# A two-layer hybrid trunk kernel on one core: first two phases pinned to the text's order, weights in idle tiles of h, GpSimd issues the later modulations' loads, TensorE makes one part of them

## The chip, the cores and the metric

The kernel runs on one core of one Trainium2 chip. The metric is device time in microseconds (us), the median over several runs; one further run was taken with the profiler and left the trace that is read here.

## What is computed

Two layers of a diffusion backbone, for 128 context tokens (`x_prompt`) and 256 latent tokens (`x_sample`), all in float32, width D = 2048. Each layer first makes a modulation from a condition vector (one for the context, one for the latents), then normalizes, scales and shifts its input by it, projects it, mixes, projects back and adds the result with a gate:

```python
for layer in range(DEPTH):
    sh_p, sc_p, gt_p = _adaln(c_ctx, w_mod, b_mod)       # silu(cond) @ w_mod + b_mod, split in 3
    sh_s, sc_s, gt_s = _adaln(c[:, None, :], w_mod, b_mod)
    h_p = _modulate(y_prompt, norm_g, sh_p, sc_p)        # rmsnorm(x) * (1 + scale) + shift
    h_s = _modulate(y_sample, norm_g, sh_s, sc_s)
    ...
    # layer 0: h @ l0_w_in (2048 x 7680), HGRN2 scan and dense attention, @ l0_w_out
    # layer 1: h @ l1_w_in (2048 x 5120), windowed attention, @ l1_w_out
    y_prompt = y_prompt + gt_p * out_p
    y_sample = y_sample + gt_s * out_s
```

Each modulation matrix `w_mod` is 2048 x 6144, 50 MB, and is used for two vectors only, so making a modulation is mostly a matter of loading it.

## The kernel before, in words

All 384 tokens are held together. A product `h @ w` is made in three matmuls on float32r halves (`whi` x `hh`, `whi` x `hl`, `wlo` x `hh`): the weights are loaded raw by SyncE (SP), ScalarE (ACT) rounds them to `whi`, VectorE (DVE) makes the rest `wlo`, and TensorE (PE) multiplies. `w_piece` does this for 512 KB of weights (a wlo of 128x1024).

**The start.** The first six groups of 512 columns of `l0_w_in` cannot start before the modulation of layer 0 is there. So the 16 tiles of 128 rows of h (k = 0 to 15) are taken in five phases, `START = ((0, 1), (1, 3), (3, 6), (6, 10), (10, 16))`. While the products of one phase run (`start_products`: six groups, 12 matmuls of 384 columns for each k), `start_mod` makes the modulation for the k of the next one: it loads 512 KB pieces of `l0_w_mod` (`mraw`, in the four buffers of the tag "raw"), multiplies them on PE with the two conditions (matmuls with 32 columns of weights, in four column groups of the array), copies the sums out (`ev`), transposes them, adds them up on DVE (`ms`, then `modc` and `acol`), and modulates x to `hh` and `hl` (`modulate`). These are called P0 to P4 below, P4 having 432 matmuls.

**The later modulations** (shift and scale of layer 1, the gates of both) are made by DVE in stretches of free time: `mod_acc` loads 16 pieces of 128x1024 (`mraw`, `MRAWB` = 3 buffers) and adds each in two operations, one for each condition, to `acc`; a `mod_part` then sums `acc` over the partitions on PE with four matmuls of 512 columns and four transposes. They stand in the list `mods`; `pump` runs a unit of them after each piece of weights, at `pace[1]` units a piece, when an account of DVE's and PE's time allows it. There are four parts, `mod_part(1, k0)` with k0 = 16, 24, 0, 8, then the gates.

**The order on an engine** is not that of the text: a scheduler lets each engine's instruction go when it thinks its inputs ready, with priorities. Each engine, SP and GpSimd (POOL) included, works through its queue in order, and an instruction that waits holds all behind it. POOL has the six `rpow` steps of the norms (line 444), loads of states, tables and x, and stores.

Of the kernel before, what the change touches and what calls it, by code (L numbers as in the profile page):

```python
# [14 lines left out]
P = 128  # L15
# [7 lines left out]
RATE0 = 0.6  # L23
# [22 lines left out]
def trunk_kernel(ctx: ExitStack, tc: tile.TileContext, I, O):  # L46
# [70 lines left out]
    queue, due, pace = [], [], [0.0, 0.0]  # L117

# [144 lines left out]
    def mod_acc(l, c0):  # L263
# [196 lines left out]
    def modulate(l, q, xt, rb, hq=None, parts=((0, 4),)):  # L460

        hh, hl = hq_tiles(q) if hq is None else hq
        for k0, k1 in parts:
            x = xt[:, k0:k1]
            nc.vector.tensor_tensor(out=x, in0=x, in1=rb.unsqueeze(1).broadcast_to([P, k1 - k0, T]), op=ALU.mult)
            for k in range(k0, k1):
                for c, s in CT:
                    kt = 4 * q + k
                    nc.scalar.activation(xt[:, k, s], xt[:, k, s], AF.Identity, bias=modc[l][:, kt, c:c + 1],  # L469
                                         scale=acol[l][:, kt, c:c + 1])  # L470
            nc.scalar.copy(hh[:, k0:k1], x)  # L471
            nc.vector.tensor_tensor(out=hl[:, k0:k1], in0=x, in1=hh[:, k0:k1].bitcast(F32), op=ALU.subtract)
        return hh, hl
# [232 lines left out]
    h0 = [hq_tiles(q) for q in range(4)]  # L706
# [13 lines left out]
    def start_group(acc, c0, k0, k1, copy):  # L720

        ps = [psm.tile([P, 512], F32, tag="mm", name=nm("mm")) for _ in range(4)]
        for kt, n in pairs(k0, k1):
            hi, lo = w_piece(spool, "sraw", SRAW, W0, kt, n, c0, 512)
            hh, hl = h0[kt // 4]
            for c in range(4):
                for k in range(n):
                    kq = kt % 4 + k
                    wh, wl = hi[:, k, c * P:c * P + P], lo[:, k, c * P:c * P + P]
                    nc.tensor.matmul(ps[c][:, 0:T], lhsT=wh, rhs=hh[:, kq], start=(kt + k == k0), stop=False)  # L730
                    nc.tensor.matmul(ps[c][:, 0:T], lhsT=wh, rhs=hl[:, kq], start=False, stop=False)
                    nc.tensor.matmul(ps[c][:, 0:T], lhsT=wl, rhs=hh[:, kq], start=False, stop=(kt + k == k1 - 1))
# [47 lines left out]
    for i, (k0, k1) in enumerate(phases):  # L780
# [6 lines left out]
        for j, _ in enumerate(start_products(k0, k1)):  # L787
            while done < (j + 1) * n_nxt // n:
                next(nxt, None)
                done += 1  # L790
# [462 lines left out]
```

## Time and profile before

| | us |
|---|---|
| median of 3 runs (1355.13 to 1356.93) | 1356.29 |
| the profiled execution | 1356.77 |
| its span, first to last instruction | 1355.0 |
| PE busy in the span | 1321.0 (97%) |
| DVE busy | 1019.0 (75%) |
| ACT busy | 647.9 (48%) |
| POOL busy | 72.4 (5%) |

The busy time of PE is the union of its matmuls, whose ends are modelled, so 97% says that PE rarely had nothing in flight, not that it ran at its peak. 1.8 us of the execution lie outside the span.

### The profile page before, as it was taken

To read this page: it belongs to the slowest core of one execution; us is meant where nothing else is said; L and a number is where in the kernel's file an instruction comes from. 1 tells how busy PE (TensorE), PEld (TensorE's weight loads), DVE (VectorE), ACT (ScalarE), POOL (GpSimd) and SP (SyncE) were. 2 spreads that over 40 slices of the span, in tenths; PEclk is the share of its full clock that TensorE was granted. 3 is DMA by queue.
4 is the path that set the end of the run, shared out by engine and by line. 5 is a ranking of instruction groups with operands and counts; after the bars stand their busy time and mean duration, and the time that the engine had idled before them with its cause. 6 is when DMAs were issued, how large, how long until landed. Compare 5 with 4: busy or idle time off the path is not lost.

```text
span 1355.0 us, 19101 instructions
## 1 busy us (share of the span) xinstructions
PE 1321.0 (97%) x7093; PEld 1125.7 (83%) x7093; DVE 1019.0 (75%) x1602; ACT 647.9 (48%) x1297; POOL 72.4 (5%) x84
## 2 busy tenths in 40 slices
PE   5899999999999999999999999999999999999998
PEld 4678888997888878787987887888888999998887
DVE  5678757998998745896998969995656664499743
ACT  4532233476655534755433347345766763352221
POOL 1000000000000021101000000200000101000000
PEclk8899999999999999999999999999999999999999
DMA  9989989755555334576778854784332345457642
GB/s 284 304 289 331 317 289 319 236 160 179 176 174 181 97 106 138 167 232 201 242 244 254 297 184 133 234 283 119 92 94 81 104 118 166 129 181 254 210 152 84
DMA packets 138317, 265.42 MB, mean 196 GB/s; under 512 B 8944, under 2 KB 46768, under 8 KB 138224
## 3 DMA queue, kind: packets, MB, share of 16 engines
q1 hardware_dynamic: 132592, 246.52, 56.9%
q0 software_dynamic: 5376, 17.60, 4.5%
q8 instruction: 56, 0.92, 0.3%
q14 instruction: 37, 0.30, 0.1%
q10 hardware_dynamic: 256, 0.08, 0.0%
HBM read 256.04 MB, written 8.13 MB: 195 GB/s over the span
## 4 chain that ended last, share of the span: by engine, by line
PE 91%; DMA 4%; DVE 3%; ACT 1%; POOL 1%; issue 0%; DVEq 0%; ACTq 0%; SPq 0%; POOLq 0%
PE mm L77 77%; PE px L77 14%; DMA raw<-in_l_w_in_dram 2%; DMA mraw<-in_l_w_mod_dram 1%; DVE wlo L77 1%; DVE acc L77 1%; DMA tB<-in_x_sample_dram 0%; ACT whi L370 0%; POOL sm L444 0%; DVE tB L77 0%; DMA rowc<-in_c_dram 0%; DVE tG L77 0%; ACT tE L469 0%; DVE tH L77 0%; POOL r L444 0%
## 5 line engine op out<-in xcount | busy, mean ns | idle before, releaser
L370 ACT CAST whi<-raw 128x1024 fp32r<-128x1024 f32 (+1 forms) x270 | 278.4, 1032 | 500.1 <-PE mm L77 393.7
L77 DVE TENSOR_TENSOR wlo<-raw,whi 128x1024 fp32r<-128x1024 f32 (+1 forms) x270 | 323.4, 1198 | 188.0 <-PE mm L77 148.6
L77 PE MATMUL mm<-whi,hh 128*128 128x512 f32 x1008 | 398.9, 396 | 0.0
L77 PE MATMUL mm<-wlo,hh 128*128 128x512 f32 x1008 | 391.7, 391 | 3.2 <-DVE wlo L77 3.2
L77 PE MATMUL mm<-whi,hl 128*128 128x512 f32 x1008 | 393.5, 391 | 0.6 <-DVE hl L77 0.6
L77 DVE SCALAR_TENSOR_TENSOR acc<-mraw,csil,acc 128x1024 f32<-128x1024 f32 x240 | 299.0, 1279 | 9.0 <-DMA mraw<-in_l_w_mod_dram 9.0
L77 PE MATMUL mm<-hh,whi 128*128 128x384 f32 x768 | 264.4, 347 | 7.1 <-ACT hh L471 4.6
L77 PE MATMUL mm<-hl,whi 128*128 128x384 f32 x768 | 259.2, 338 | 0.0
L77 PE MATMUL mm<-hh,wlo 128*128 128x384 f32 x768 | 254.5, 338 | 0.2 <-DVE wlo L77 0.2
L77 PEld LDWEIGHTS mm<-wlo,hh 128*128 128x128 f32 x1008 | 189.3, 188 | 42.7 <-DVE wlo L77 5.8
L77 PEld LDWEIGHTS mm<-whi,hl 128*128 128x128 f32 x1008 | 189.3, 188 | 40.8 <-DVE hl L77 1.5
L77 PEld LDWEIGHTS mm<-whi,hh 128*128 128x128 f32 x1008 | 189.4, 188 | 39.3 <-ACT tE L824 0.8
L77 PEld LDWEIGHTS mm<-hh,whi 128*128 128x128 f32 x768 | 145.3, 190 | 22.2 <-issue 10.1
L77 PEld LDWEIGHTS mm<-hh,wlo 128*128 128x128 f32 x768 | 144.8, 189 | 2.7 <-DVE wlo L77 1.0
L77 PEld LDWEIGHTS mm<-hl,whi 128*128 128x128 f32 x768 | 145.5, 190 | 1.2 <-issue 0.2
L623 ACT ACTIVATE p<-px,nb,rs 128x384 f32<-128x384 f32 (+1 forms) x72 | 42.4, 596 | 15.0 <-DVE nb L77 14.5
L77 PE MATMUL px<-mraw,cs 128*32 128x256 f32 (+1 forms) x576 | 40.4, 377 | 4.9 <-DMA mraw<-in_l_w_mod_dram 4.9
L633 ACT ACTIVATE p<-p,sum 128x384 f32<-128x384 f32 (+1 forms) x72 | 36.1, 540 | 15.1 <-DVE sum L77 13.2
L77 DVE TENSOR_REDUCE mx<-px 128x1 f32<-128x384 f32 (+1 forms) x54 | 29.7, 567 | 9.3 <-PE px L77 8.9
L77 PEld LDWEIGHTS px<-mraw,cs 128*32 128x32 f32 x576 | 16.3, 114 | 20.0 <-issue 8.2
L77 PEld LDWEIGHTS px<-ct,p 128*128 128x128 f32 x168 | 20.1, 141 | 8.3 <-issue 2.8
L444 POOL TENSOR_TENSOR rs<-rs,nhalf 128x12 f32<-128x12 f32 x6 | 14.7, 2450 | 227.5 <-DVE rs L77 227.5
(415 smaller groups left out, 1228.5 us busy)
## 6 DMA issues: line engine op xcount, KB each, us to landing
raw<-in_l_w_in_dram SPq DMA_DIRECT2D x194, 512.0 KB, 3.9
mraw<-in_l_w_mod_dram SPq DMA_DIRECT2D x192, 512.0 KB, 5.0
raw<-in_l_w_out_dram SPq DMA_DIRECT2D x64, 512.0 KB, 4.9
raw<-in_l_w_in_dram SPq DMA_DIRECT2D x12, 256.0 KB, 6.6
tK<-in_l_b_mod_dram POOLq DMA_DIRECT2D x6, 256.0 KB, 6.0
y1d<-tA POOLq DMA_DIRECT2D x2, 768.0 KB, 5.2
tD<-y1d POOLq DMA_DIRECT2D x2, 768.0 KB, 6.0
tL<-y1d POOLq DMA_DIRECT2D x2, 768.0 KB, 6.2
```

What stands on the lines that cost most here:

```text
L77: return f(*a, **k)
L370: nc.scalar.copy(hi, raw)
L444: nc.gpsimd.tensor_tensor(out=out, in0=out, in1=nhalf[:, 0:out.shape[1]], op=ALU.pow)
L623: nc.scalar.activation(p[:, j], ss[j], AF.Exp, bias=nb[:, j:j + 1], scale=rs[:, i + j:i + j + 1], accum_out=sm[:, j:j + 1])
L633: nc.scalar.activation(p[:, j], p[:, j], AF.Copy, scale=sm[:, j:j + 1])
```

## The change

Seven things change. `pin` keeps P0's and P1's matmuls on PE and weight loads on SP (with the modulation work that runs beside them, that is of k = 0 to 5) in the order of the text. The eight modulation pieces of k = 1, 2 go to the six idle tiles of h and two of the four "raw" buffers. The multiplication of x with `rb0` stands ahead, and `modulate` works on one k at a time; for a phase's first k ACT writes `hh` straight from x. `pace[1]` is 0 in P0. The last piece of modulation work of a phase comes one or two pieces of weights earlier (`n`). `mod_acc` loads are issued by POOL, inside `tc.issue_after(last_w[0].ins)`. And `mod_part(1, 8)` on DVE is replaced by `late_mod(1, 8)` on PE, beside P4's products.

```diff
-RATE0 = 0.6
+RATE0 = (0.0, 0.6, 0.6, 0.6, 0.6)
...
+    def pin(ins, queue):
+
+        if pinned[queue]:
+            tc.keep_in_program_order(ins)
+        return ins
...
             raws.append(wpool.tile([P, 1024], F32, tag="mraw", bufs=MRAWB, name=nm("mraw")))
-            nc.sync.dma_start(raws[kt], I[f"l{l}_w_mod"][kt * P:kt * P + P, c0:c0 + 1024])
+
+            with tc.issue_after(last_w[0].ins):
+                nc.gpsimd.dma_start(raws[kt], I[f"l{l}_w_mod"][kt * P:kt * P + P, c0:c0 + 1024])
...
-        nc.sync.dma_start(raw, w_view(w, kt, nk, c0, n))
+        ins = pin(nc.sync.dma_start(raw, w_view(w, kt, nk, c0, n)), "s")
+        if pinned["s"]:
+            last_w[0] = ins
...
+    def modulate(k, first):
+
+        x, (hh, hl) = xT[k // 4][:, k % 4], [t[:, k % 4] for t in h0[k // 4]]
+        for c, s in CT:
+            m, a = modc[0][:, k, c:c + 1], acol[0][:, k, c:c + 1]
+            nc.scalar.activation(hh[:, s] if first else x[:, s], x[:, s], AF.Identity, bias=m, scale=a)
+            if first:
+                nc.vector.tensor_scalar(out=x[:, s], in0=x[:, s], scalar1=a, scalar2=m, op0=ALU.mult, op1=ALU.add)
+        if not first:
+            nc.scalar.copy(hh, x)
+        return nc.vector.tensor_tensor(out=hl, in0=x, in1=hh.bitcast(F32), op=ALU.subtract)
...
-    h0 = [hq_tiles(q) for q in range(4)]
+
+    h0 = [hq_tiles(0)]
+    done0 = []
+    idle = ["hh1", "hl1", "hh2", "hl2", "hh3", "hl3"]
...
-                    raw = wpool.tile([P, k8, n], F32, tag="raw", bufs=RAWB, name=nm("mraw"))
-                    nc.sync.dma_start(raw, w_view(I["l0_w_mod"], k8 * i, k8, D * (1 - part) + k * P, n))
+                    if k == 1 and idle:
+                        raw = hpool.tile([P, 4 * T], F32, tag=idle.pop(0), name=nm("mraw"))[:, 0:1024]
+                        raw = raw.rearrange("p (k c) -> p k c", k=k8)
+                    else:
+                        raw = wpool.tile([P, k8, n], F32, tag="raw", bufs=RAWB, name=nm("mraw"))
+                    pin(nc.sync.dma_start(raw, w_view(I["l0_w_mod"], k8 * i, k8, D * (1 - part) + k * P, n)), "s")
...
+    def late_mod(l, k0):
+
+        for k in (k0, k0 + 4):
+            ps = px()
+            for i in range(8):
+                raw = wpool.tile([P, 2, 512], F32, tag="raw", bufs=RAWB, name=nm("mraw"))
+                nc.sync.dma_start(raw, w_view(I[f"l{l}_w_mod"], 2 * i, 2, k * P))
+                for kt in (2 * i, 2 * i + 1):
+                    nc.tensor.matmul(ps[32 * (kt % 4):32 * (kt % 4) + 32, :],
+                                     lhsT=cs32[:, kt, :], rhs=raw[:, kt % 2], start=(kt < 4), stop=(kt >= KT - 4))
+                yield
+            ev = mpool.tile([P, 512], F32, tag="t2", bufs=T2B, name=nm("ev"))
+            nc.scalar.copy(ev, ps)
+            cp = px()
+            for b in range(4):
+                nc.tensor.transpose(cp[:, b * P:b * P + P], ev[:, b * P:b * P + P], ident)
...
-    mods += [mod_part(1, k0) for k0 in (16, 24, 0, 8)] + [mod_gates(0, 0, "KL", ready0)]
-    pace[1] = RATE0
+    mods += [mod_part(1, k0) for k0 in (16, 24, 0)] + [mod_gates(0, 0, "KL", ready0)]
+    pinned["t"] = pinned["s"] = True
...
+            nxt, n_nxt = late_mod(1, 8), 16
+
+        n = len(first) * len(pairs(k0, k1)) - (2 if i == 0 else 1)
```

What this makes of the engines' queues is seen at three places. The first is the head of POOL's queue. Before, it holds three small loads and then the power step of the first norm (`r_239`), which all of the start waits for:

```order
L205 DMA rowb<-in_lb_gamma_dram 48x128
L219 DMA onh<-in_l_a_onorm_dram 128x1
L221 DMA nsink<-in_l_c_sink_dram 128x16
L444 ISA
L444 TENSOR_TENSOR r_239<-r_239,nhalf 128x1 x3
```

Of the change, the same place:

```order
L282 DMA mraw_677<-in_l_w_mod_dram 128x1024
L282 DMA mraw_679<-in_l_w_mod_dram 128x1024
L282 DMA mraw_796<-in_l_w_mod_dram 128x1024
L214 DMA rowb<-in_lb_gamma_dram 48x128
L228 DMA onh<-in_l_a_onorm_dram 128x1
L230 DMA nsink<-in_l_c_sink_dram 128x16
L282 DMA mraw_910<-in_l_w_mod_dram 128x1024
L457 ISA
L457 TENSOR_TENSOR r_239<-r_239,nhalf 128x1 x3
L282 DMA mraw_1015<-in_l_w_mod_dram 128x1024
```

The loads of the first later part stand at the very head, four of them before the norm's power step; the `issue_after` that names a load of SP has put none of them behind anything on POOL.

The second place is DVE from the sums of the first modulation (`ms`, k = 0) to the first `hl`, which P0's matmuls need. Before:

```order
L77 TENSOR_REDUCE ms_314<-px_311 128x4
L77 TENSOR_TENSOR wlo_332<-raw_328,whi_330 128x512
L77 TENSOR_TENSOR modc_122<-ms_314,par 128x2 x2
L77 TENSOR_TENSOR tG_187<-tG_187,rb_238 128x768
L77 SCALAR_TENSOR_TENSOR acol_124<-modc_122,par 128x2
L77 TENSOR_TENSOR tH_217<-tH_217,rb_238 128x768
L77 TENSOR_TENSOR wlo_365<-raw_361,whi_363 128x512
L77 TENSOR_TENSOR tH_217<-tH_217,rb_238 128x768
L77 TENSOR_TENSOR hl_43_255<-tE_133,hh_42_254 128x384
```

Of the change:

```order
L77 TENSOR_REDUCE ms_309<-px_306 128x4
L77 SCALAR_TENSOR_TENSOR acc_676<-mraw_1015,csil,acc_676 128x1024
L77 TENSOR_TENSOR modc_122<-ms_309,par 128x2 x2
L77 SCALAR_TENSOR_TENSOR acc_676<-mraw_1015,csil,acc_676 128x1024
L77 SCALAR_TENSOR_TENSOR acol_124<-modc_122,par 128x2
L77 SCALAR_TENSOR_TENSOR acc_676<-mraw_1093,csil,acc_676 128x1024
L77 TENSOR_SCALAR tE_133<-tE_133,acol_124,modc_122 128x128
L77 SCALAR_TENSOR_TENSOR acc_676<-mraw_1093,csil,acc_676 128x1024
L77 TENSOR_SCALAR tE_133<-tE_133,acol_124,modc_122 128x256
L77 SCALAR_TENSOR_TENSOR acc_676<-mraw_1269,csil,acc_676 128x1024
L77 TENSOR_TENSOR hl_43_255<-tE_133,hh_42_254 128x384
```

Five `acc` operations of a later part have moved in between; in the whole queue of the change all 32 of that part stand before the 12th `wlo`, the end of P1's, where before they were spread from the 4th to the 29th.

The third place is PE in P4, where one piece of weights ends and the next begins. Before:

```order
L77 MATMUL mm_2095<-hh_48_260,whi_2128 128x384
L77 MATMUL mm_2095<-hl_49_261,whi_2128 128x384
L77 MATMUL mm_2095<-hh_48_260,wlo_2130 128x384
L77 MATMUL mm_2092<-hh_48_260,whi_2162 128x384
L77 MATMUL mm_2092<-hl_49_261,whi_2162 128x384
```

Of the change:

```order
L77 MATMUL mm_2100<-hh_344_1866,whi_2135 128x384
L77 MATMUL mm_2100<-hl_345_1867,whi_2135 128x384
L77 MATMUL mm_2100<-hh_344_1866,wlo_2137 128x384
L77 MATMUL px_2163<-mraw_2164,cs_109 32x512 x2
L77 MATMUL mm_2097<-hh_344_1866,whi_2170 128x384
L77 MATMUL mm_2097<-hl_345_1867,whi_2170 128x384
```

Two matmuls of `late_mod` stand between the pieces, and so 16 times in P4, with four transposes after the 8th and the 16th time.

## Rows read from the trace of the kernel before

**Rows 1.** The page, part 1: busy us (share), instructions.
```profile
PE 1321.0 (97%) x7093; PEld 1125.7 (83%) x7093; DVE 1019.0 (75%) x1602; ACT 647.9 (48%) x1297; POOL 72.4 (5%) x84
```
**Rows 2.** Stretches: length, busy of each engine, PE clock, DMA share, GB/s.
```profile
core 0: us, PE busy (x) PEld busy (x) DVE busy (x) ACT busy (x) POOL busy (x), PEclk, DMA share, GB/s
30.00:215.00 185.00, 175.62 (x1268) 144.13 (x1261) 125.05 (x193) 65.10 (x103) 0.60 (x1) 0.97 0.93 309
...
215.00:290.00 75.00, 75.00 (x433) 74.99 (x433) 71.20 (x75) 41.51 (x50) 1.43 (x2) 1.00 0.70 231
290.00:1355.00 1065.00, 1054.44 (x5267) 895.24 (x5265) 803.37 (x1286) 528.58 (x1113) 66.77 (x71) 1.00 0.55 172
```
**Rows 3.** The chain that ended last, pieces: start us, us, what.
```profile
30.50 7.64 PE mm L77 x36
...
57.97 11.24 PE mm L77 x48
...
87.33 4.11 PE mm L77 x22
...
214.79 107.85 PE mm L77 x576
...
289.96 32.68 PE mm L77 x144
```
**Rows 4.** Order of time, PE alone, around a `mod_part`'s four matmuls.
```profile
322.25 0.39 PE L77 MATMUL mm<-whi,hl 128*128 128x512 f32 x1
322.57 1.07 PE L77 MATMUL px<-acc,ct 128*32 128x512 f32 x8
323.57 0.50 PE L77 MATMUL mm<-whi,hh 128*128 128x512 f32 x1
323.90 0.39 PE L77 MATMUL mm<-wlo,hh 128*128 128x512 f32 x1
```
**Rows 5.** The same around eight matmuls of `start_mod`, and its transposes.
```profile
147.90 0.34 PE L77 MATMUL mm<-hh,wlo 128*128 128x384 f32 x1
148.17 1.07 PE L77 MATMUL px<-mraw,cs 128*32 128x256 f32 x16
149.17 0.44 PE L77 MATMUL mm<-hh,whi 128*128 128x384 f32 x1
...
213.16 0.66 PE L77 MATMUL px<-ct,ev 128*128 128x128 f32 x4 [0.71 <-ACT ev L756]
```
**Rows 6.** DVE's work on `mraw` until 345 us: ns min/median/max.
```profile
L77 DVE SCALAR_TENSOR_TENSOR acc<-mraw,csil,acc x69: 1273/1279/1286, 36.0 to 340.2; 128x1024 f32<-128x1024 f32 x69
```
**Rows 7.** Stretches of the front, columns as in Rows 2.
```profile
0.00:20.00 20.00, 10.77 (x55) 8.10 (x55) 10.32 (x33) 9.31 (x26) 3.58 (x10) 0.98 0.94 273
20.00:26.00 6.00, 4.02 (x69) 3.08 (x73) 5.14 (x9) 1.37 (x3) 0.00 (x0) 0.77 0.76 222
...
64.00:72.00 8.00, 8.00 (x73) 7.46 (x73) 5.97 (x10) 1.32 (x2) 0.29 (x1) 1.00 0.29 89
72.00:92.00 20.00, 19.76 (x149) 16.48 (x151) 16.00 (x28) 5.28 (x7) 0.31 (x1) 1.00 1.00 343
```
**Rows 8.** The loads of `mod_acc` until 92 us, on SP's queue.
```profile
L271 SPq DMA_DIRECT2D mraw<-in_l_w_mod_dram x7: 367/477/1356, 25.1 to 71.4; - x7
```
**Rows 9.** Order of time, DVE: sums of k = 0, then its `hl`.
```profile
25.28 0.17 DVE L77 TENSOR_REDUCE ms<-px 128x4 f32<-128x16 f32 x1
...
29.38 0.55 DVE L77 TENSOR_TENSOR hl<-tE,hh 128x384 fp32r<-128x384 f32 x1
```
**Rows 10.** Loads of 256 KB on SP's and POOL's queue: median us to landing.
```profile
raw<-in_l_w_in_dram SPq DMA_DIRECT2D x12, 256.0 KB, 6.6
...
mkf<-in_masks_dram POOLq DMA_DIRECT2D x1, 256.0 KB, 6.6
```
**Rows 11.** The chain that ended last, from 290 to 490 us, by engine and line.
```profile
by line: PE mm L77 78.0%; PE px L77 22.1%
```
**Rows 12.** A stretch of the first layer's output projection, columns as in Rows 2.
```profile
700.00:760.00 60.00, 57.89 (x263) 46.47 (x262) 54.78 (x58) 24.92 (x45) 5.10 (x8) 1.00 0.81 255
```

More of the change, by code (lines that the diff above doesn't have):

```diff
@@ L744, in start_mod @@
             ps = px()
+            for i in range(k, k + nk):
+                x = xT[i // 4][:, i % 4]
+                if k:
+                    with tc.issue_after(done0[0].ins):
+                        nc.vector.tensor_tensor(out=x, in0=x, in1=rb0, op=ALU.mult)
+                else:
+                    nc.vector.tensor_tensor(out=x, in0=x, in1=rb0, op=ALU.mult)
             for part in range(2):
                 for i in range(2 * nk):
-                    raw = wpool.tile([P, k8, n], F32, tag="raw", bufs=RAWB, name=nm("mraw"))
-                    nc.sync.dma_start(raw, w_view(I["l0_w_mod"], k8 * i, k8, D * (1 - part) + k * P, n))
+                    if k == 1 and idle:
+                        raw = hpool.tile([P, 4 * T], F32, tag=idle.pop(0), name=nm("mraw"))[:, 0:1024]
+                        raw = raw.rearrange("p (k c) -> p k c", k=k8)
+                    else:
+                        raw = wpool.tile([P, k8, n], F32, tag="raw", bufs=RAWB, name=nm("mraw"))
+                    pin(nc.sync.dma_start(raw, w_view(I["l0_w_mod"], k8 * i, k8, D * (1 - part) + k * P, n)), "s")
                     for j in range(k8):
                         kt = k8 * i + j
-                        nc.tensor.matmul(ps[32 * (j % 4):32 * (j % 4) + 32, part * n:part * n + n],
-                                         lhsT=cs32[:, kt, :], rhs=raw[:, j], start=(kt < 4), stop=(kt >= KT - 4))
+                        pin(nc.tensor.matmul(ps[32 * (j % 4):32 * (j % 4) + 32, part * n:part * n + n],
+                                             lhsT=cs32[:, kt, :], rhs=raw[:, j], start=(kt < 4), stop=(kt >= KT - 4)), "t")
                     if part == 0 or i < 2 * nk - 1:
@@ L766, in start_mod @@
                 mod_cols(0, KT * (1 - part) + k, nk, sums[:, nk * part:nk * part + nk, :])
[L767 to L768 removed]
+            for i in range(k, k + nk):
+                if len(h0) <= i // 4:
+                    h0.append(hq_tiles(i // 4))
+                m = modulate(i, i == k0)
+                done0.append(m)
+            yield
+    def late_mod(l, k0):
[7 more added lines that the diff above has]
+                                     lhsT=cs32[:, kt, :], rhs=raw[:, kt % 2], start=(kt < 4), stop=(kt >= KT - 4))
+                yield
+            ev = mpool.tile([P, 512], F32, tag="t2", bufs=T2B, name=nm("ev"))
[3 more added lines that the diff above has]
+                nc.tensor.transpose(cp[:, b * P:b * P + P], ev[:, b * P:b * P + P], ident)
+            sums = spool.tile([P, 8], F32, tag="ms", bufs=2, name=nm("ms")).rearrange("p (b c) -> p b c", c=2)
+            nc.vector.tensor_reduce(
+                out=sums, in_=cp.rearrange("p (b j r) -> p b r j", j=4, r=32)[:, :, 0:2, :], axis=AX.X, op=ALU.add)
+            mod_cols(l, k, 4, sums)
     def start_products(k0, k1):
@@ L783, in trunk_kernel @@
             k2, k3 = phases[i + 1]
-            nxt, n_nxt = start_mod(k2, k3), 4 * (k3 - k2)
-        n = len(first) * len(pairs(k0, k1))
+            nxt, n_nxt = start_mod(k2, k3), 4 * (k3 - k2) + len(pairs(k2, k3))
+        else:
+            nxt, n_nxt = late_mod(1, 8), 16
+        n = len(first) * len(pairs(k0, k1)) - (2 if i == 0 else 1)
         done = 0
         for j, _ in enumerate(start_products(k0, k1)):
-            while done < (j + 1) * n_nxt // n:
+            while done < min(n_nxt, (j + 1) * n_nxt // n):
                 next(nxt, None)
```

26 lines of the change are left out of this document (8 added, 18 removed).

## The prediction

> **What bounds the kernel now.** I read the page's busy times first: TensorE 97%, VectorE 75% [rows 1]. A modelled 97% could still hide waits, so next come the stretches. From 290 us to the end TensorE is idle for 1065 - 1054.4 = 10.6 us, at full clock [rows 2]; from 290 to 490 us the chain is its matmuls and nothing else, 78.0% and 22.1% [rows 11]. In P4 it is never idle, and its rate shows: the 576 matmuls from 214.79 take 107.85 us, the last 144 of them, of 512 columns, 32.68, so the 432 of P4 take 75.2 us, 0.174 us each [rows 3]. Whatever is put into P4 on TensorE lengthens the kernel by its own time.
>
> Only the front is different. The first product starts at 30.5 us, P1 at 57.97, P1's last ones end at 91.4, P4 starts at 214.79 [rows 3]. Until 92 us the transfers are nearly full: 273 GB/s in the first 20 us, 343 at the end, with two holes, 222 GB/s from 20 to 26 and 89 from 64 to 72 [rows 7]. From 30 to 215 TensorE is idle for 9.4 us, and the clock averages 0.97 of 2.4 GHz, a loss of about 5.6 us [rows 2]. So the front has transfers and TensorE both close to their limit, with some 15 us to be had at most, and everything behind it is TensorE alone.
>
> **The change part by part.** *One part on TensorE (`late_mod`).* 16 times two matmuls of 512 columns stand between pieces of weights in P4. The trace has four such matmuls together, one in each column group: the last product before them starts at 322.25, the next behind at 323.57, 1.32 us instead of 0.227 (32.68/144 [rows 3]); the one after that is late by another 0.10 (0.33 instead of 0.227) [rows 4]. That is 1.19 us for four. Are two half of that? The four go as two passes of 0.43 us in which all groups run side by side (eight records in 1.07 us [rows 4]; sixteen of half the columns also in 1.07 [rows 5]); two matmuls still need both passes. I take the whole 1.19, with half of it, 0.6, as the lower bound: 16 x 1.19 = 19.0. Two times four transposes at 0.66 [rows 5] make 1.3. Together **+20.4 us**, bounds 10.9 and 20.4. Nothing covers it, as TensorE has no gap in P4. Could transfers make it more? P4 would load 9.4 MB of weights, 8.4 of late pieces and up to 8.4 for VectorE's next part, 26.2 MB in 75 + 20 us, 276 GB/s, where 343 is seen [rows 7]; I add nothing.
>
> What it replaces is `mod_part(1, 8)`: on TensorE 1.19 + 0.66, **-1.9 us**; on VectorE 32 operations, 2 of them cheaper, at 1.28 us [rows 6], 41 us. What are those 41 us worth? VectorE is 75% busy and TensorE waits little: of the 10.6 us idle behind 290 us, the clearest part is in the output projection, 60 - 57.9 = 2.1 us from 700 to 760, where VectorE is busy for 54.8 of 60 us [rows 12], because the gates are finished at the last moment. With one part less in the list they come a part earlier, so I take **-2.1 us**; bounds 0 (other work is moved into the same place) and -10.6 (all idle time behind 290 goes).
>
> *The front.* POOL issues the later loads, and nothing holds them: three stand at the head of its queue, 1.57 MB, which go beside x. At 273 GB/s [rows 7] x is whole 5.8 us later, and so are the norm and all behind it. Then VectorE has five `acc` operations, 6.4 us, between `ms` and the first `hl`, where before it had about 4.1 us from 25.28 to 29.38 with other work [rows 9]: +2.3. So the first product comes near 30.5 + 8 = 38.5 us. Each of these five also waits for its load, and the power step of the norm stands behind the fourth load on POOL; I see nothing that makes these later than the transfers themselves.
>
> By the end of P1 the change has to move: x and constants 3.5 MB, modulation for six k 12.6, weights of three k 4.7, and all 16 loads of the first later part 8.4 (before, seven had been issued by 92 us [rows 8]): 29.2 MB. 5.5 MB go in the first 20 us, the other 23.7 at 343 GB/s take 69 us [rows 7]: 89 us, and the last pieces still have to be multiplied, some 4 us: 93. This assumes that the idle h tiles and the text's order fill the holes, worth 0.7 and 2.0 MB. TensorE from 38.5: 216 products at 0.174 are 37.6 us; 16 modulation loads of k = 1, 2, 4, 5 at 1.10 us for two (149.17 - 147.90 less 0.17 [rows 5]) 8.8; k = 3 half of four such, 2.2 with its start; transposes 2.0: 50.6, ending at 89 without any stall. Both limits lie close together, near 91.4 us of before; I take 93 to 94, +2. In P2 and P3 the later loads of before are gone and the last piece of modulation work comes a piece of weights earlier, which closes the gap ahead of P4 in part: -1. **Front +1 us**; bounds -15 (all idle time and slow clock of 30 to 215 given back) and +14 (nine more loads of 0.524 MB at 343 GB/s, no hole filled).
>
> A rule of the Trainium skill speaks against POOL's loads: by DMA: Bandwidth & Descriptors, section Queues, rings and completion order, each transfer engine goes round between the queues that have work, a packet from each, so that a second busy queue would get up to half. Here a load of 256 KB from POOL landed in 6.6 us, just as the 256 KB loads on SP's full queue did, 6.6 [rows 10], which does not show a POOL load overtaking. I go by the row; the rule's result is a rival.
>
> The other edits cost nothing that I can see: the split of `modulate` into single k is ACT and VectorE work, both with room (ACT 48%), and covered by P2's and P3's products; without that cover it would be some tenths of a us a phase.
>
> **Sum.** Against the profiled execution of 1356.77, which is 0.5 us over the median: 1356.8 + 20.4 - 1.9 - 2.1 + 1.0 = **1374 us**.
>
> **The rivals.** *Forecast:* P4 pays in full and the front comes out even: 1374, with its own range 1367 to 1381.
>
> *POOL's loads take the front.* If they get half of the transfers while they last, 16 loads are through after 8.4 MB at 171 GB/s, 49 us, in which SP's queue moves 8.4 MB; it needs 10.8 for the modulation of k = 1, 2 and P0's weights, so these land near 59 us, P1 starts near 66 instead of 58 and ends near 99: +7.6 instead of +2 there. 1380; with no hole filled, 1387. For it: three loads ahead of x, VectorE in order behind them. Against: rows 10. This is where the skill's rule above would lead.
>
> *Two matmuls cost half of four.* 10.9 instead of 20.4: 1365. For it only that the records are half as many; against, that the passes, not the records, took the time.
>
> *Faster: the front gives back more than P4 takes.* The place is P0 and P1: six pieces loaded into idle tiles while P0's weights run, so that SP's queue is never stuck on the four "raw" buffers, and products in the text's order, so that P1 need not wait from 50 to 58 us. From 30.5 to 91.4 are 61 us for 50.6 of work, so 10 us are there; 5 more could come from P2 and P3, and up to 10.6 behind 290. 1356.8 + 20.4 - 1.9 - 15 - 10.6 = 1350. It decides where P4 starts: with 18.5 us net paid in it and 2.1 got back later, before 198 us instead of 214.8 the kernel is faster. Against: the later first product takes 8 us of these first.
>
> *The change does not do what it says.* For POOL's `issue_after` that is so, as the queue shows, and is in the sum; had it held the loads back until P0's weights are under way, the front would be near -5 and the time 1368, inside the range.
>
> **How the numbers follow.** The forecast has 0.62, POOL's loads taking the front 0.15, half cost 0.10, and the faster case with all between it and no change 0.13. The range of 1362 to 1385 holds the forecast, the half cost and most of the second case, and leaves out the last and the worst fronts. A measurement of this kernel can tell about 0.2%, 2.7 us. Slower by more has all of the first three, 0.87; the last 0.13 I split into 0.08 faster and 0.05 the same.
>
> **What would show each step.** P4, from its first product to the last one of 384 columns, should take 94 to 96 us instead of 75.2, with 16 pairs of modulation matmuls about 1.2 us apart from the products around them. The three `mraw` loads should be issued on POOL by 3 us, the last load of x land near 21 us, the first product start at 37 to 40 us, P1 end at 91 to 97, P4 start at 212 to 220. All 32 `acc` operations of the first part should be done by P1's end. TensorE's idle time from 700 to 760 should fall under 1 us, and 290 to 490 us stay as dense as before. The prediction is wrong if P4's pairs cost well under 1 us, if P4 starts before 205 us, or if VectorE, waiting for POOL's loads, holds up P0 beyond 45 us.

## The result, and the profile after

The changed kernel took 1398.76 us (median of 4 runs, 1397.27 to 1401.89) against 1356.61 us before: 1.031 times as long, 95% interval 1.0282 to 1.0337. That is 42 us more, where 1374 had been forecast, with 1385 as the upper end. The profiled execution (1401.89, span 1400.1 us) is 45.1 us longer than that of before, and its stages say where; it is the slowest of the four, so the stages add up to 3 us more than the medians differ by. The front, up to P4's first product, went from 214.8 to 230.7 us, +15.9. P4 went from 75.2 to 96.1 us, +20.9. From P4's last product to the end it took 1073.2 instead of 1065.0 us, +8.2. One of these three terms, P4, came out as forecast.

The stretches of the changed kernel, columns as in [rows 2] and [rows 7], which they answer:

```profile
0.00:20.00 20.00, 9.50 (x44) 7.80 (x44) 8.94 (x22) 9.50 (x26) 4.13 (x11) 1.00 0.94 300
20.00:41.00 21.00, 6.51 (x78) 4.42 (x76) 16.31 (x33) 3.42 (x8) 6.32 (x7) 0.63 1.08 354
41.00:69.00 28.00, 21.63 (x141) 16.26 (x141) 22.79 (x35) 15.50 (x32) 2.65 (x5) 0.85 0.88 285
69.00:83.00 14.00, 11.53 (x78) 11.07 (x79) 11.71 (x18) 2.48 (x5) 1.06 (x2) 0.76 0.46 151
83.00:114.00 31.00, 25.68 (x202) 21.25 (x200) 24.82 (x43) 8.66 (x14) 2.65 (x5) 0.94 0.99 341
231.00:327.00 96.00, 96.00 (x515) 77.98 (x514) 77.46 (x84) 41.67 (x48) 7.57 (x15) 1.00 0.75 253
327.00:1400.00 1073.00, 1055.03 (x5258) 896.74 (x5256) 766.20 (x1255) 534.28 (x1118) 118.51 (x152) 1.00 0.52 162
737.00:797.00 60.00, 56.91 (x250) 46.72 (x249) 53.28 (x51) 20.65 (x34) 11.62 (x21) 0.97 0.82 273
```

In P4 TensorE is never idle, as before: its price is its own work. Behind P4 it idles for 1073 - 1055.0 = 18 us where it was 10.6 [rows 2], and the stretch around the gates, which was to lose its idle time, has 3.1 us instead of 2.1 [rows 12]. In the front the transfers run at 341 to 354 GB/s in two stretches, at 285 from 41 to 69 us and at 151 from 69 to 83 us. The last of these is a hole like that of 64 to 72 us before [rows 7]: against 343 GB/s it lacks 2.7 MB, where the one before lacked 2.0. The granted clock of 20 to 41 us, a mean of 0.63 between its two levels (1.2 and 2.4 GHz) with TensorE busy for 6.5 of 21 us, goes with the late start; what it cost is not separated.

The chain that ended last, pieces of the front (start us, us, what):

```profile
26.69 12.69 DMA raw<-in_l_w_in_dram
39.40 0.62 ACT whi L383
40.02 0.41 ACT hh L478
...
55.98 9.27 DMA raw<-in_l_w_in_dram
...
69.76 1.19 DVE acc L77
70.95 0.48 DVE hl L77
...
96.19 1.20 DVE acc L77
97.39 0.23 DVE tD L77
97.62 7.83 DMA raw<-in_l_w_in_dram
```

Three loads of weights that land 8 to 13 us after their issue, an `hh` that stands behind the cast of such a load on ScalarE, and sums of the later part (`acc`) between TensorE's results and the next `hl`. The chain of before had one such load in the front, of 7.83 us, and 3.3 us of sums, nearly all of them behind 69 us.

The same bytes went to another use. The queues until 91.4 us, the end of P1 before, first of the kernel before and then of the changed one (packets, MB, share of 16 engines; q1 is SP's, q0 POOL's):

```profile
q1 hardware_dynamic: 23652, 26.49, 90.3%
q0 software_dynamic: 176, 0.30, 0.9%
```
```profile
q1 hardware_dynamic: 18430, 17.65, 61.9%
q0 software_dynamic: 2388, 8.40, 25.2%
```

Both moved 26 to 27 MB. POOL moved 8.1 MB more than before, all of it for the later part, and SP's queue 8.8 MB less. By 113.9 us, when P1 ends, SP has 23.65 MB and POOL 10.26. From 20 to 41 us alone, in the changed kernel:

```profile
q1 hardware_dynamic: 6162, 5.32, 81.7%
q0 software_dynamic: 576, 2.10, 26.4%
```

### The profile page after: what moved, and what is told of

It reads as the page before. It is cut to its first block, busy times and chain, and to the rows that moved or that the text cites. A ratio compares the mean times of both kernels' runs of the same rounds, so it can differ in the third digit from the quotient of the medians.

```text
span 1400.1 us, 19251 instructions
## 1 busy us (share of the span) xinstructions
PE 1341.1 (96%) x7153; PEld 1132.6 (81%) x7153; DVE 990.1 (71%) x1597; ACT 654.3 (47%) x1306; POOL 142.9 (10%) x196
## 4 chain that ended last, share of the span: by engine, by line
PE 87%; DMA 4%; DVE 4%; issue 1%; ACT 1%; SPq 1%; POOL 1%; DVEq 0%; POOLq 0%; ACTq 0%
PE mm L77 73%; PE px L77 14%; DMA raw<-in_l_w_in_dram 2%; DMA mraw<-in_l_w_mod_dram 1%; DVE acc L77 1%; DVE wlo L77 1%; SPq L773 1%; DMA tA<-in_x_sample_dram 1%; POOL rs L457 0%; ACT whi L383 0%; DVE tB L77 0%; POOL sm L457 0%; SPq L379 0%; DVE hl L77 0%; DVE tE L77 0%
## 5 line engine op out<-in xcount | busy, mean ns | idle before, releaser
L77 PE MATMUL mm<-hh,whi 128*128 128x384 f32 x768 | 268.0, 349 | 11.8 <-ACT hh L478 8.7
L77 DVE SCALAR_TENSOR_TENSOR acc<-mraw,csil,acc 128x1024 f32<-128x1024 f32 x210 | 262.2, 1277 | 7.3 <-DMA mraw<-in_l_w_mod_dram 7.1
L77 PE MATMUL mm<-hh,wlo 128*128 128x384 f32 x768 | 260.5, 339 | 1.5 <-DVE wlo L77 1.5
L77 PEld LDWEIGHTS mm<-hh,whi 128*128 128x128 f32 x768 | 145.8, 190 | 38.4 <-ACT whi L383 11.4
L282 POOL DMA_DIRECT2D mraw<-in_l_w_mod_dram x112 | 60.2, 538 | 664.8 <-DVE acc L77 626.0
L77 PE MATMUL px<-mraw,cs 128*32 128x256 f32 (+2 forms) x640 | 53.5, 405 | 1.1 <-DMA mraw<-in_l_w_mod_dram 1.1
L633 ACT ACTIVATE p<-px,nb,rs 128x384 f32<-128x384 f32 (+1 forms) x72 | 42.4, 596 | 12.7 <-DVE nb L77 12.1
L457 POOL TENSOR_TENSOR rs<-rs,nhalf 128x12 f32<-128x12 f32 x6 | 20.9, 3482 | 155.3 <-DVE rs L77 154.8
```

The lines of the kernel that those rows point to most:

```text
L77: return f(*a, **k)
L282: nc.gpsimd.dma_start(raws[kt], I[f"l{l}_w_mod"][kt * P:kt * P + P, c0:c0 + 1024])
L457: nc.gpsimd.tensor_tensor(out=out, in0=out, in1=nhalf[:, 0:out.shape[1]], op=ALU.pow)
L633: nc.scalar.activation(p[:, j], ss[j], AF.Exp, bias=nb[:, j:j + 1], scale=rs[:, i + j:i + j + 1], accum_out=sm[:, j:j + 1])
```

## The experiments

Stages of every run, from its trace, in us: start of the first product, end of P1's last, start of P4, length of P4, from there to the end; then the median time. The ratio to the kernel before, run beside it, follows with its interval.

| run | first | P1 end | P4 start | P4 | behind | median | ratio |
|---|---|---|---|---|---|---|---|
| before | 30.4 | 91.4 | 214.8 | 75.2 | 1065.0 | 1356.6 | |
| changed | 41.0 | 113.9 | 230.7 | 96.1 | 1073.2 | 1398.8 | 1.031 (1.028-1.034) |
| e1 | 41.3 | 112.9 | 229.2 | 76.7 | 1082.3 | 1393.4 | 1.028 (1.025-1.030) |
| e2 | 29.7 | 89.4 | 209.9 | 95.2 | 1061.5 | 1368.7 | 1.010 (1.008-1.012) |
| e3 | 26.0 | 87.3 | 215.3 | 96.1 | 1063.4 | 1376.7 | 1.016 (1.014-1.019) |
| e4 | 26.6 | 86.9 | 214.1 | 96.2 | 1076.1 | 1389.4 | 1.024 (1.022-1.027) |
| e5 | 39.1 | 103.5 | 218.1 | 96.5 | 1062.9 | 1381.6 | 1.019 (1.017-1.021) |
| e6 | 32.9 | 95.7 | 211.0 | 96.1 | 1073.0 | 1382.7 | 1.021 (1.018-1.023) |
| e7 | 41.1 | 111.9 | 226.5 | 96.1 | 1072.0 | 1395.2 | 1.029 (1.027-1.031) |
| e8 | 26.8 | 91.5 | 225.4 | 75.0 | 1081.8 | 1380.9 | 1.019 (1.017-1.021) |
| e9 | 41.6 | 115.4 | 230.6 | 89.5 | 1071.2 | 1395.1 | 1.028 (1.027-1.030) |
| e10 | 39.3 | 124.1 | 235.5 | 96.1 | 1069.3 | 1405.3 | 1.036 (1.034-1.038) |
| e11 | 40.9 | 113.2 | 228.6 | 96.1 | 1065.7 | 1392.0 | 1.026 (1.024-1.028) |
| e12 | 30.0 | 90.6 | 210.9 | 89.0 | 1061.4 | 1362.5 | 1.004 (1.003-1.006) |
| e13 | 40.9 | 110.4 | 226.2 | 96.1 | 1070.3 | 1393.8 | 1.028 (1.026-1.029) |
| e14 | 25.6 | 91.3 | 217.2 | 89.5 | 1065.8 | 1373.9 | 1.013 (1.010-1.015) |
| e15 | 29.3 | 89.5 | 213.6 | 75.2 | 1065.7 | 1356.3 | 1.000 (0.999-1.001) |

**late_mod taken out, and alone (e1, e2).** Taken out of the changed kernel:

```diff
-    mods += [mod_part(1, k0) for k0 in (16, 24, 0)] + [mod_gates(0, 0, "KL", ready0)]
+    mods += [mod_part(1, k0) for k0 in (16, 24, 0, 8)] + [mod_gates(0, 0, "KL", ready0)]
...
-            nxt, n_nxt = late_mod(1, 8), 16
```

> The changed kernel without late_mod: k = 8 to 15 go back to mod_part, as a fourth later part on VectorE. Theory (P4 paid 20.9 us because every pair of modulation matmuls costs TensorE its full two passes): P4 takes 75 to 76 us instead of 96.1, mod_part's matmuls come back (+1.9), P4 still starts near 231; 1398.8 - 20.9 + 1.9 = 1380, plus 0 to 3 for one more part on VectorE. Rival (P4 is slow because weights, late pieces and POOL's loads fight for the transfers): P4 stays above 80 us and the time above 1385.

P4 fell to 76.7 us as the theory said, and only 5 us of it reached the end: behind P4 1082.3 instead of 1073.2 us. The fourth part came back to VectorE, where the parts already ran late, and the gates of the output projection were waited for. What TensorE waited for behind P4 (total us, times, longest):

```profile
PE px L77 <- ACT ahi L336: 9.7, 1, 9.7
PE mm L77 <- DVE tF L77: 1.9, 1, 1.9
PE mm L77 <- DVE gt L77: 1.9, 1, 1.9
```

The price of P4 was right, the theory's total (1380 to 1383) missed; the rival's (above 1385) came out, but not by its cause, since P4 did fall below 80 us. Next `late_mod` alone in the kernel before (the function added, `(16, 24, 0)` in `mods`, and 16 of its steps in P4):

> The kernel before with late_mod alone (SP's queue, no idle tiles, no written order). Theory: P4 grows from 75.2 to 95.5 us, mod_part goes (-1.9), TensorE's waits for wlo behind P4 stay at 2 to 4 us: 1356.6 + 20.5 - 1.9 = 1375, and the other half of the loss (16 us ahead of P4, 8 behind it) is not late_mod's. Rival (late_mod also causes the waits behind P4, since the other parts lie differently on VectorE): 1380 or more, with 8 to 10 us of waits for wlo behind P4.

P4 paid 20.0 us, and 7.9 of it came back: 4.9 ahead of P4, which starts earlier, and 3.5 behind it, together 8.4 in the two profiled executions. The 288 products from the 2592nd on, in which the gates come due, took 68.0 us instead of 73.3. So `late_mod` costs 12 us by itself, less than the theory's 18 and without the rival's waits. The other 30 come with the rest of the change.

**POOL's loads (e3, e4).** In e3 the loads of `mod_acc` go on SP's queue again, where `issue_after` holds them; in e4 they stay on POOL behind two copies that need a cast piece of P2's weights, and no unit of the later parts runs in P1 either (`RATE0`).

```diff
-                nc.gpsimd.dma_start(raws[kt], I[f"l{l}_w_mod"][kt * P:kt * P + P, c0:c0 + 1024])
+                nc.sync.dma_start(raws[kt], I[f"l{l}_w_mod"][kt * P:kt * P + P, c0:c0 + 1024])
```

> The changed kernel with the later modulations' loads on SP's queue again, where issue_after holds them behind the first weights. Theory A (POOL's loads take transfers from the front and come late behind P4): P1 ends near 95 to 100 instead of 113.9, P4 starts at 214 to 220 instead of 230.7, TensorE's waits for wlo behind P4 fall from 10.3 to about 3 us; 1377 to 1382. Theory B (the written order is slow by itself: TensorE's modulation matmuls stand in the text's place, so SP's loads wait for their buffers): P1 ends at 108 or later, P4 starts at 226 or later; 1390 or more.

```diff
-RATE0 = (0.0, 0.6, 0.6, 0.6, 0.6)
+RATE0 = (0.0, 0.0, 0.6, 0.6, 0.6)
...
+    last_hi, hold0 = [None], [0]
...
+            if hold0[0] < MRAWB - 1:
+                hold0[0] += 1
+                nc.gpsimd.tensor_copy(raws[kt][0:1, 0:1], last_hi[0])
...
+        last_hi[0] = hi[0:1, 0, 0:1].bitcast(F32)
```

> The changed kernel with POOL's loads still on POOL's queue, but the first two behind a copy of one element of a cast piece of P2's weights, so that the first later part starts near P1's end. Theory A (the bytes of the later part in the front are what it costs): first product near 37 us, P1 ends at 92 to 98, P4 starts at 212 to 219; 1382 to 1388, with the waits behind P4 as they were or longer. Theory B (the written order is slow by itself): P1 ends at 108 or later, P4 starts at 225 or later; 1395 or more.

In the front both runs decide for theory A, and went further than it said (P1's end at 92 to 100 us; for e4 a first product near 37 us). The first product starts at 26 us, 15 earlier than in the changed kernel and 4 earlier than before; P1 ends at 87, 27 earlier. What the written order with its idle tiles does by itself until P1's end is not separated by these 4 us: by then the kernel before has issued 7 loads and made 14 sums of the later parts, e3 5 and 8, e4 3 and none. At P4's start 15 to 17 of the 27 us are left, as the loads and sums come in P2 and P3 instead: from P1's end to P4's start e3 and e4 take 128 and 127 us, the changed kernel 117, the one before 123. No run came to P4 more than 4.9 us earlier than before (e2). That a later part costs about the same ahead of P4 wherever it is put is read from this and not shown: no run leaves it out there. In total e4 missed by a little (1389.4 for 1382 to 1388), as its later parts end later and the stretch behind P4 takes 1076.1 us.

**Loads or sums (e5, e6).** Loads and sums stand in the front together; each was taken out alone. From the second load on e5 leaves out 992 of the 1024 columns of each sum, and e6 loads 2 of the 16 pieces; both leave that part of the modulation incomplete.

```diff
-                    nc.vector.scalar_tensor_tensor(out=acc[:, c], in0=raw, scalar=s, in1=acc[:, c],
+                    w = 32 if (l, c0) == (1, 16 * P) else 1024
+                    nc.vector.scalar_tensor_tensor(out=acc[:, c, 0:w], in0=raw[:, 0:w], scalar=s, in1=acc[:, c, 0:w],
```

> The changed kernel, but the sums of the first later part take 32 columns instead of 1024 from its second load on (that part of the modulation is left out). All its loads stay on POOL's queue. Theory A (the loads take the transfers of the front): first product at 37 to 41 us, P1 ends at 108 us or later, P4 starts at 224 us or later. Theory C (VectorE's sums of 1.28 us, which stand ahead of hl and wlo, hold the front): first product below 34 us, P1 ends before 98, P4 starts before 218.

```diff
+            if (l, c0) == (1, 16 * P) and kt > 1:
+                raws.append(raws[0])
+                return
```

> The changed kernel, but the first later part loads two pieces only and makes all of its 32 sums of 1024 columns from these (14 of 16 pieces of the modulation's weights are left out). Theory A (transfers): first product at 28 to 33 us, P1 ends at 87 to 95, P4 starts at 210 to 218. Theory C (VectorE's sums ahead of hl and wlo): first product at 36 us or later, P1 ends at 105 or later.

The loads are the larger part, but not the only one. Without them the first product comes 8.0 us earlier, P0 takes 24.1 us instead of 27.5 and P1 38.7 instead of 45.4, so that P1 ends 18.2 and P4 starts 19.7 us earlier (in part because 7.3 MB are never loaded). Without the sums the first product comes only 1.9 us earlier (39.1) and P0 is 0.9 shorter, but P1 takes 37.9 us, and P4 starts 12.6 earlier. So the loads cost in all three places, the sums nearly only in P1. At P1's end the two gains, 18.2 and 10.4, make 28.6 us; e4, which moves all sums and nearly all loads behind P1, gained 27.0, and e3, which leaves 5 loads and 8 sums there, 26.6.

**The queue behind P4 (e7, e8).** In e7 only the first later part loads on POOL; e8 is e3 without `late_mod`.

```diff
-                nc.gpsimd.dma_start(raws[kt], I[f"l{l}_w_mod"][kt * P:kt * P + P, c0:c0 + 1024])
+                eng = nc.gpsimd if (l, c0) == (1, 16 * P) else nc.sync
+                eng.dma_start(raws[kt], I[f"l{l}_w_mod"][kt * P:kt * P + P, c0:c0 + 1024])
```

> The changed kernel with POOL's queue for the first later part alone; the parts behind it load on SP's queue. The front should be as in the changed kernel (P4 starts at 228 to 233). Theory (behind P4 a load on POOL is issued late, behind POOL's other work, and lands late against SP's): from P4's end to the end 1062 to 1066 us instead of 1073.2, waits for wlo there 2 to 4 instead of 10.3; 1387 to 1391. Rival (VectorE is late because the first parts end late, the queue doesn't matter): 1071 to 1075 us behind P4, 1397 to 1400.

1072.0 us behind P4: my theory fell, and the queue makes little difference there. P4 started at 226.5 us, earlier than the 228 to 233 named, and the median lies between theory and rival.

> The changed kernel with the later loads on SP's queue and without late_mod: what is left of the change is the written order and the idle tiles. If P4's cost comes back whole: 1376.7 - 20.9 + 1.9 = 1358, and up to 1366 where the fourth part makes VectorE late behind P4. Rival (as without late_mod alone, where only 5.4 us came back, since the part then lands late on VectorE): 1370 or more.

The rival held, and more: P3 took 82.9 us instead of 71.5 before, and behind P4 there is the wait for the gates of e1 again (9.8 us). e8 has neither `late_mod` nor POOL's loads, and is still 25.5 us slower than the kernel before that ran beside it: what is left of the change costs that by itself, in the profiled executions 10.6 us ahead of P4 and 16.7 behind it. With `late_mod` in place the same rest costs 8 us (e3 against e2). The third part's sums run at 483 to 572 us in e8, before at 324 to 421; which of the remaining edits moves them back was not tried.

**The price of a piece (e9, e12).** The pieces of `late_mod` as four matmuls of 256 columns, in the changed kernel and in that of before:

```diff
-                raw = wpool.tile([P, 2, 512], F32, tag="raw", bufs=RAWB, name=nm("mraw"))
-                nc.sync.dma_start(raw, w_view(I[f"l{l}_w_mod"], 2 * i, 2, k * P))
...
+                raw = wpool.tile([P, 4, 256], F32, tag="raw", bufs=RAWB, name=nm("mraw"))
+                h, i4 = i // 4, 4 * (i % 4)
+                nc.sync.dma_start(raw, w_view(I[f"l{l}_w_mod"], i4, 4, k * P + 256 * h, 256))
...
```

> The changed kernel with the pieces of late_mod cut as 4 x 256 columns instead of 2 x 512: four matmuls of 256 columns, one in each column group, for the same bytes. Theory (the two passes over a piece's columns are what is paid, and groups run side by side): a piece costs 0.55 us, as start_mod's, instead of 1.2; P4 takes 85 to 87 us instead of 96.1; 1388 to 1390. Rival (the price is the switch between products and px matmuls, twice per piece): P4 stays at 92 us or more; 1395 or more.

TensorE in order of time around one piece, changed kernel and then e9:

```profile
238.89 0.34 PE L77 MATMUL mm<-hh,wlo 128*128 128x384 f32 x1
239.15 1.05 PE L77 MATMUL px<-mraw,cs 128*32 128x512 f32 x4
240.14 0.45 PE L77 MATMUL mm<-hh,whi 128*128 128x384 f32 x1
240.42 0.34 PE L77 MATMUL mm<-hl,whi 128*128 128x384 f32 x1
```
```profile
254.82 0.34 PE L77 MATMUL mm<-hh,wlo 128*128 128x384 f32 x1
255.09 0.64 PE L77 MATMUL px<-mraw,cs 128*32 128x256 f32 x8
255.65 0.45 PE L77 MATMUL mm<-hh,whi 128*128 128x384 f32 x1
255.94 0.34 PE L77 MATMUL mm<-hl,whi 128*128 128x384 f32 x1
```

From the product ahead to the next 1.25 us and 0.83, less 0.174 of its own, and 0.1 more behind: a piece costs 1.18 us, and 0.77 with half the columns. Half the columns save 0.41, so if the price is a fixed part and one by columns, about 0.36 are paid for the change between products and modulation, whatever is in it; that is an estimate from two sizes. Theory and rival each had one part of the price. P4 fell by 6.6 us to 89.5, the median by 3.7; the two ratios' intervals overlap, so the saving is clear in P4's length, not in the total.

> The kernel before with late_mod alone, its pieces cut as 4 x 256 columns. If a piece costs half: P4 at 85 to 86 us instead of 95.2, 1368.7 - 9.8 = 1359, within 1357 to 1361: about what the gain ahead of and behind P4 pays for. If not: 1365 or more.

P4 takes 89.0 us and the kernel 1362.5, between the two expectations: the nearest of those with `late_mod`, still 6 us slower than before.

**ScalarE's order (e10, e11).** In e10 the casts `whi` of P0 and P1 keep the text's order.

```diff
-        nc.scalar.copy(hi, raw)
+        pin(nc.scalar.copy(hi, raw), "t")
```

> The changed kernel with the casts of whole pieces (whi) of P0 and P1 kept in the text's order on ScalarE, so that the first hh no longer stands behind the cast of a later piece whose load has not landed. Theory (this order is the part of the late first product that the loads ahead of x do not explain): first product at 38 to 39.5 us instead of 41.0, P1's end and P4's start 2 to 6 us earlier; 1393 to 1397. Rival (transfers set P1's end whatever the first product does): first product earlier, P1 still ends at 112 to 115; 1397 to 1400.

The first product came 1.7 us earlier, as the theory said, and P1 ended 10 us later, as neither did. What TensorE waited for from 20 to 125 us in e10:

```profile
PE mm L77 <- ACT whi L383: 21.6, 6, 8.8
```

The longest of the six is the wait for the first product itself. Two more, 4.4 us together at 64 and 70 us, end with casts that ScalarE reached behind evictions, the copies of P0's finished sums (`tK`, `tL`). The other three, 8.3 us together, end with casts behind an `hh` and behind a piece that landed late; so the evictions are a part of what P1 lost, not all of it.

In e11 the exponentials and logarithms of `hgrn_prep` and `hgrn_decay` keep the text's order, each issued behind the one before:

```diff
-            nc.scalar.activation(e, e, AF.Exp)
+            act(e, e, AF.Exp)
...
+            with tc.issue_after(last_a[0].ins):
+                last_a[:] = [nc.scalar.activation(*a, **kw)]
...
```

> The changed kernel with the exponentials and logarithms of hgrn_prep and hgrn_decay kept in the text's order on ScalarE (5 loads of an activation table instead of 13). Theory (the first 4 us lost behind P4 are table loads of 1.28 us in the chain to tB and tD): the 96 products from the 1200th on take 22 to 24 us instead of 26.9, and nothing else changes; 1393 to 1396. Rival (VectorE is late there in any case): 1397 to 1400.

The theory held for the 96 products, and the total was better than expected: 6.8 us faster than the changed kernel, and behind P4 1065.7 us, what it took before. ScalarE in the changed kernel, where the chain runs through it:

```profile
336.60 1.28 ACT L920 ACT_TABLE_LOAD   x1
337.89 0.22 ACT L920 ACTIVATE dd<-hg 128x12 f32<-128x12 f32 x1
...
339.99 1.28 ACT L883 ACT_TABLE_LOAD   x1
341.29 0.62 ACT L883 ACTIVATE tB<-tB,ct 128x384 f32<-128x384 f32 x1
...
344.58 1.28 ACT L921 ACT_TABLE_LOAD   x1
...
346.42 1.28 ACT L883 ACT_TABLE_LOAD   x1
...
348.34 1.28 ACT L922 ACT_TABLE_LOAD   x1
...
351.11 1.28 ACT L882 ACT_TABLE_LOAD   x1
```

Exponentials of one head and logarithms of the next group alternate, and each change loads a table for 1.28 us. From the 1200th to the 1296th product the changed kernel took 26.9 us, before 22.9, e11 21.8. The place of the loads decides, not their number: e2, e3 and e12 also load 13 tables in all, but at most 3 of them start in this stretch, and it takes 22.2 to 23.0 us. Over all runs it takes 21.8 to 23.0 us with 0 to 3 loads in it, 26.2 with 4 (e4), 26.9 to 27.1 with 5 and 29.6 with 6 (e9). So 5.1 of the 7.5 us that e11 wins behind P4 are won where the table loads were. Another 2.1 come from the 1872nd to the 2016th product, and e9 with 17 loads is as short there: their cause stays open. The waits behind P4, changed kernel and then e11:

```profile
PE mm L77 <- DVE wlo L77: 10.3, 6, 3.4
```
```profile
PE mm L77 <- DVE wlo L77: 3.5, 3, 2.5
```

The wait is put down to VectorE, since `wlo` stands behind a product with `tB` on VectorE, which waits for ScalarE: the engine named is not the one that is late.

**Few buffers, the sum of the savings, and the order by itself (e13, e14, e15).**

```diff
-                        raw = wpool.tile([P, k8, n], F32, tag="raw", bufs=RAWB, name=nm("mraw"))
+                        ring[0] += 1
+                        pool, tag, bufs = (spool, "mfront", 1) if ring[0] % 5 == 0 else (wpool, "raw", RAWB)
+                        raw = pool.tile([P, k8, n], F32, tag=tag, bufs=bufs, name=nm("mraw"))
```

> The changed kernel with a fifth buffer for start_mod's pieces of the modulation: every fifth of those that go into raw gets a tile of its own. Theory (stalls of TensorE become holes in the transfers, because the next piece can only be loaded when TensorE has used up one of four buffers): the holes near 50 and 70 us get shorter, P1 ends 2 to 6 us earlier than 113.9, P4 starts at 225 to 229; 1393 to 1397. Rival (bytes alone set P1's end): P1 ends at 112 to 115, P4 starts at 229 to 232; 1397 to 1400.

What SP's queue waited for from 20 to 115 us, changed kernel and then e13:

```profile
SPq L773 <- PE px L77: 32.9, 8, 13.7
```
```profile
SPq L775 <- PE px L77: 23.7, 5, 12.3
```

P1 ended 3.5 us earlier and P4 started 4.5 earlier, as the theory had it; the median fell by 4.9, with intervals that just overlap. The wait for used-up buffers became shorter by 9 us in sum, the longest one, at the hole near 70 us, by 1.4. Two things weaken it. Kernels with the same front ended P1 at 112.9 to 115.4 us (e1, e9, e11, one profiled execution each), and e7 started P4 at 226.5 us without a fifth buffer, so that little of the difference may be e13's own. And in the kernel before, without the written order, SP's queue waited for used-up buffers as long, from 20 to 92 us:

```profile
SPq L748 <- PE px L77: 35.0, 11, 10.7
```

So a fifth buffer may help a little; that the written order makes these waits is not shown.

> The changed kernel with the three edits that helped: later loads on SP's queue, late_mod's pieces as 4 x 256 columns, ScalarE's exponentials and logarithms in the text's order. If the savings add up: 1376.7 - 6.6 (P4) - 0 to 3 (behind P4, where the loads on SP had left little to win) = 1367 to 1370, still slower than before by the rest of late_mod. If they do not add up: 1371 or more.

They do not add up: 1373.9. P1 ended 4 us later than in e3, and the order on ScalarE gave nothing behind P4, where e3 had lost nothing.

> The kernel before with ScalarE's exponentials and logarithms in the text's order (5 table loads instead of 7), nothing of the change. In the changed kernel this order left the stretch from the 1200th to the 1296th product shorter than before by 1 us and the one behind it by 0.8. Theory: 1354.5 to 1356, a gain too small to tell. Rival (the order delays work that now runs early): 1358 or more.

1356.3, ratio 1.0002 (0.9991 to 1.0013): no gain by itself. e11 undid what the change had moved. None of these kernels beats the one before. One way from it to the changed kernel, by medians, is 12 us for `late_mod` (e2), 8 more for the rest of the change with the loads on SP (e3), and 22 for putting these on POOL; without `late_mod` the middle step costs 25 (e8), so the steps depend on each other.

## Why the prediction was wrong

**Right: P4.** 20.4 us had been put on `late_mod`, at 1.19 us a piece and 1.3 for transposes; P4 grew by 20.9, a piece costs 1.18, and nothing covers it. The rival with half the price fell: two matmuls in two column groups cost what four in four groups did [rows 4]. The price does not go by the number of matmuls; by the estimate from e9 it has a fixed part of 0.36 us and 0.41 for every 256 columns of a group.

**Failed, and the largest: the front, +1 forecast, +15.9 measured, above its bound of +14.** P1 was to end at 93 to 94 and ended at 113.9. The step that failed is "29.2 MB ... the other 23.7 at 343 GB/s", in both of its factors. By P1's end 34.1 MB had gone: 19 loads of the later parts instead of 16, and weights of P2. And they had gone at a mean of (34.1 - 6.0)/93.9 = 299 GB/s. "I see nothing that makes these later than the transfers themselves" was the sentence behind it. Two things did, and both belong to the later part. Its loads take the transfers (e6: P1 ends 18.2 us earlier without them), and its sums stand on VectorE ahead of `hl` and `wlo` (e5: 10.4 us). VectorE itself waited only 1.6 us for these loads from 20 us to P1's end, so the waiting for them is a small part of it, and their bytes, which SP's queue lacked, the likely rest. With both moved behind P1 (e4), or most of them (e3), the loss is gone and P1 ends 4 us earlier than before. The first `hh`, which stands behind the cast of a piece that lands after 12.7 us, is worth 1.7 us at the first product (e10). I had booked the written order and idle tiles as filling holes of 0.7 and 2.0 MB; with POOL's loads the hole from 69 to 83 us alone lacks 2.7 MB. Behind P1 6.6 us came back, where 1 had been forecast. How far the loads' and the sums' shares depend on each other stays open, as does what the written order adds to the loss when POOL's loads are there.

The rival "POOL's loads take the front" had the place and the cause, not the size: it gave +7.6 us at P1's end, where 22.5 were lost. Against it I had set one landing time [rows 10]. That row is of a single load, issued at 71.7 us at the end of the hole [rows 7], and does not say how the bytes of two full queues divide. In the changed kernel a POOL load of 512 KB issued at 26.6 us landed after 8.2 us, the 256 KB load that SP issued at 26.7 us after 12.7. The 10.8 MB of this rival are not only what it names, 4.2 MB of modulation and 1.6 of weights; with x and the modulation of k = 0 these come to 11.4. From 20 to 41 us POOL moved 2.10 of 7.43 MB, and until 91.4 us its 8.40 MB displaced SP's one for one. The Trainium skill, DMA: Bandwidth & Descriptors, section Queues, rings and completion order, has the transfer engines go round between queues with work; the trace agrees in kind, with a share of 28 to 32% for POOL, whose loads wait for `acc` in between, rather than half.

**Failed: "the other edits cost nothing that I can see".** By it the pace and the one-k `modulate` stood at nothing; the written order and idle tiles stood in the front as a help, and for none of them was anything counted on VectorE behind P1. With the loads on SP they cost together 8 us where `late_mod` is there (e3 against e2), and some 25 us where it is not (e8). e8 shows where: VectorE's later parts run later, and the gates are waited for. Which edit does it stays open.

**Failed: behind P4, -4.0 forecast with the removed matmuls, +8.2 measured.** The -2.1 for gates that come a part earlier is right for `late_mod` alone: e2 took 5.3 us less for those products. In the changed kernel they took 73.0 us, no less than before. The third part's sums had moved back (498 to 597 us, before 324 to 421), and those of the second gate ended 57 us behind the 2592nd product, in e2 35 and before 94. The wait of 3.1 us there is for a `wlo` behind a sum on VectorE, and the chain runs through that sum's load, which POOL issued behind a store and two loads of x:

```profile
762.04 10.58 DMA mraw<-in_l_w_mod_dram
```

With those loads on SP the products took 71.8 us (e7). The other part was not in my list at all: another order on ScalarE, with 5 table loads instead of 1 in the chain's 96 products. That is 4.0 of the 8.2 us; e11, which takes out all 5, gives back 7.5, of which 5.1 there; what else makes up the 8.2 stays open.

**The signs that had been named.** The three loads left POOL between 1.3 and 3.0 us; the last load of x was issued at 10.85 and landed 7.8 us later, near 18.6 instead of 21; the first product came at 41.0, just outside 37 to 40; the first part's 32 sums ended at 103 us, before P1's end. P1's end and P4's start lay outside the 91 to 97 and 212 to 220 us that had been named.

The faster rival asked for P4 before 198 us. The earliest of all runs was 209.9.

## What to carry to other kernels

A load that is put on an idle queue is not free where transfers are the limit: it takes the bytes from the queue that the bound engine waits for (8.1 MB more on POOL, 8.8 less on SP). Sum up bytes per queue until the end of each phase, and look which loads have no hold: here the hold named an instruction of another engine and held nothing.

An engine pinned to the written order waits for whatever stands ahead in the other queues: here sums on VectorE (7.5 us of P1, e5) and a cast on ScalarE (1.7 us, e10). Before pinning, follow what each in-order queue (casts, sums, buffer releases) has in front of the instruction that the pinned engine needs next, and look at the stages behind as well: e8 ended P1 as early as the kernel before and lost some 25 us behind it.

A change far ahead can reorder an engine that it never touches. Compare the order of every engine behind the change too, above all instructions that only a change of order makes, like table loads, and whether they fall where another engine waits.

## What the runs showed of the hardware that was not expected

- A table load on ScalarE takes 1.283 us each of 13 times, and the next activation starts 0.01 us behind it (336.60 + 1.28, 337.89). ScalarE: Activation LUTs of the Trainium skill, section Table sets: the hidden batching unit, advises to batch by set; the trace agrees, with 26.9 us against 21.8 for the same 96 products between the changed kernel and e11. The section also counts one load for a logarithm and then an exponential, as one of its sets holds both; here every change between the two loaded a table, as the rows of ScalarE show.
- Two queues with loads of 512 KB share: POOL's 8.4 MB of 26 until 91.4 us came off SP's 26.5 nearly byte for byte. The first five weights pieces of 256 KB on SP landed after 7.5 to 12.7 us, before after 4.8 to 9.6.
- A lone piece of modulation between products costs an estimated 0.36 us beside its columns (1.18 and 0.77 us for 512 and 256 columns a group); two pieces together, sixteen records, cost 1.10 [rows 5], where two lone ones of that size cost 1.54.
